# Second-layer attention of a hybrid decoder: which engine copies the turned tiles, how the projections are split, and a fourth output row begun early

## The chip, the cores and the metric

The kernel runs on one core of a Trainium2 chip. The metric is the device time of one execution in microseconds (us). The core's engines each have a queue of instructions that they take in order: PE (TensorE: matmuls, and transposes as matmuls), DVE (VectorE), ACT (ScalarE), POOL (GpSimd) and SP (SyncE, which here only issues transfers). An instruction that waits for a semaphore holds up all that stands behind it on its engine.

## The reference

The reference is a decoder of two layers on 512 tokens of width 1024: a gated delta-rule layer, then a layer with sliding-window attention. What matters here is the second layer's mixer and the output projection behind it:

```python
proj = h @ swa_w_q[bl]
q = apply_partial_rope(proj[..., :SWA_Q_W].reshape(b_sz, s_len, SWA_HEADS, SWA_DH), cos, sin)
mix_out = sliding_window_attention(q, shared_k, shared_v, swa_sinks[bl])
mem_q = proj[..., SWA_Q_W:]
...
mem_o = memory_attention(mem_q.reshape(b_sz, s_len, MEM_HEADS, MEM_DH), mem_k, mem_v)
x = x + jnp.concatenate([mix_out.astype(x.dtype), mem_o.astype(x.dtype)], axis=-1) @ w_out[layer]
x = x + swiglu(rms_norm(x, ln_ffn[layer]), w_gate_up[layer], w_down[layer])
```

and inside the attention, per block of 128 queries against the 256 keys of its own and the preceding block, twelve query heads on two key heads:

```python
m = jnp.maximum(jnp.max(s, axis=-1, keepdims=True), sink)
p = jnp.exp(s - m)
p = (p / (jnp.sum(p, axis=-1, keepdims=True) + jnp.exp(sink - m))).astype(v.dtype)
o = jnp.einsum("bnhgqk,bnkhd->bnqhgd", p, vw)
```

The memory attention has four heads and 256 fixed tokens, with no sinks.

## The kernel before

Activations lie with features on the 128 partitions and the 512 tokens along the free axis. A dense product is made exact to nearly float32 from rounded halves: `split` gives a high half (a copy on ACT, `whi`, `h`) and a low half (a subtraction on DVE, `wlo`, `l`), and `mm3` does three matmuls for each 128-row step k: high by high, high by low, low by high. So an output tile of 128x512 takes 8 steps or 24 matmuls, and every weight tile of 128x1024 is loaded to `wraw` by SP (two buffers), then split by ACT and DVE (three buffers `whi`/`wlo`) before PE can use it. A weight load waits until the tile that had its `wraw` buffer two loads earlier has been split.

The second layer's mixer is `swa`. Eight items t go through it: six head pairs (t = 0 to 5) and two pairs of memory heads (t = 6, 7). For each, `queries(t)` projects (24 matmuls into a `pj` bank of PSUM), `score(t)` makes the scores of four query blocks n = 0 to 3 into `qk` allocations of two banks each and DVE takes the maxima, `softmax(t)` makes the exponentials on ACT (for head pairs first the sinks' `es`, then eight of them into `sm`) and `weighed` scales and turns the probabilities and multiplies by the values. PSUM's eight banks are held as two `pj`, two `qk` allocations of two banks, and two `pt`.

`weighed` goes over the four blocks n. It scales the two halves b = 0, 1 of the block by the reciprocal of the sum (DVE for even n, ACT for odd n), turns the tile on PE into a `pt` bank (up to four 128x128 transposes), and copies the bank to SBUF as `pf`: on ACT, for n = 2 on DVE (L822). With all four turned, 28 matmuls (for memory items 4 wide ones) multiply by the values into another `pt` bank, and `split` of that bank gives the item's mix, `h` and `l`. It yields after n = 1 and n = 3, and ends with the product.

`beside(t, work)` drives `weighed` in three steps and puts dense work on PE in front of each: two k-steps of a projection (six matmuls), three times, so that PE has something to do while ACT and DVE scale and copy. The last two of the eight steps of the projection come after. In the loop's last two rounds and behind it, the dense work is that of the output projection: `row(1, m, ...)` is output tile m as a chain of eight steps in the order of items 6, 7, 0, 1, 2, 3, 4, 5, of which the last needs the mix of item 5. Rows 0, 1 (in `pj`) and 2 (in one half of a `qk` allocation) are begun in the attention. `output` then finishes these, makes the other rows (banks `pj`, `pj`, `pt` in turn, by m % 3), and behind each row adds it to the residual tile (`x`, on DVE), splits the result scaled by the gain as input of the feed-forward, and adds its square to the sum for the norm.

The feed-forward `ffn` starts with `gate(0)`: 24 matmuls into a `pj` bank. Its later tiles come in pairs by a scheme of seven products for eight, `quarters`, for which sums of weight tiles are needed: two `ws` loads of 256 KB on SP (L1020, L1021), onto which POOL adds two more of 256 KB by adding transfers (L1022, L1023), and a `wraw` load of 256 KB (L1025). `token_sums` makes sums of the inputs (`fc`, `raw`, `T`).

The order on each engine is not that of the Python code alone: the program's builder places instructions ahead where their inputs allow, loads and splits above all, keeping dependencies, buffers and the edges that `nosync` adds (an order on one engine without a semaphore). In the built program, loads and splits of rows 3 and 4 lie ahead of the end of the attention, and the `ws` loads of the feed-forward too.

Of the kernel before, what the change touches and what calls it, by code (L numbers as in the profile page):

```python
# [12 lines left out]
AF = mybir.ActivationFunctionType  # L13
ALU = mybir.AluOpType
# [4 lines left out]
P = 128  # L19
# [66 lines left out]
class Builder:  # L86
    def __init__(self, tc, a):
        self.tc, self.nc, self.a = tc, tc.nc, a
        self.n = 0
        self.valued = None  # L90
        self.table, self.table_ins, self.table_users = None, None, []


# [17 lines left out]
    def bank(self, tag, shape=(P, T)):  # L111
        return self.t(self.pp, list(shape), F32, tag, self.pbufs[tag])
# [278 lines left out]
    def gates(self, ep):  # L391
# [34 lines left out]
        self.mm(pg[:, NH:2 * NH], self.ones, g2)  # L426
        row = self.t(ep, [NH, P], F32, "row")
        self.copy(row, pg[:NH, 64:64 + P])
        dr = self.t(self.dpool, [1, NH * P], F32, "dr")
        nc.sync.dma_start(dr.rearrange("o (n i) -> (o n) i", i=P), row)  # L430
        self.dr = dr
        self.ngc = self.t(self.mpool, [P, NH], F32, "ngc")
# [356 lines left out]
    def weighed(self, pool, scores, vv, m, out, win):  # L789

        nc = self.nc
        own = "pt" in self.pbufs
        half = [slice(0, 64), slice(64, P)]
        sm, mx, den, nm = scores
        o = None if own else self.bank("sc")
        group = NC if own else 2
        for n in range(NC):
            if n % group == 0:
                pf = {} if win else self.t(pool, [P, 2, 2, group * P], F32, "pfm" if own else "pf", 1)
            k0 = 1 if win and n == 0 else 0  # L800
            p = sm[n][:, :, k0 * P:]
            dn = den.rearrange("p (b n) -> p n b", b=2)[:, n, :]
            for b in range(2):
                if n % 2:
                    self.copy(p[:, b], p[:, b], scale=dn[:, b:b + 1])
                else:
                    self.ts(p[:, b], p[:, b], dn[:, b:b + 1], ALU.mult)
            pt = self.bank("pt" if own else "g", [P, 2, 2, P])
            for j in range(k0, 2):
                for b in range(2):  # L810
                    turned = self.tr(pt[:, j, b, :], sm[n][:, b, j * P:(j + 1) * P])
                    if self.ahead is not None:

                        self.nosync(turned, self.ahead)
                        self.ahead = None
            if win:
                pf[n] = self.t(pool, [P, 2, 2, P], F32, "pf", group)
                to = pf[n][:, k0:]
            else:
                to = pf[:, :, :, n % group * P:(n % group + 1) * P]  # L820
            if own and n == 2:
                nc.vector.tensor_copy(to, pt[:, k0:])  # L822
            else:
                self.copy(to, pt[:, k0:])
            if own and n % 2:
                yield
            if (n + 1) % group:
                continue
            if own:
                o = self.bank("pt")  # L830
            if win:
                parts = [(t[:, j, b, :], vv[n - 1 + j][:, half[b]], slice(n * P, (n + 1) * P), j if n else 0, j, b)
                         for n, t in pf.items() for j in range(0 if n else 1, 2) for b in range(2)]
            else:
                parts = [(pf[:, j, b, :], vv[j][:, m * P + 64 * b:m * P + 64 * b + 64],
                          slice((n + 1 - group) * P, (n + 1) * P), j, j, b) for j in range(2) for b in range(2)]
            for t, v, s, first, end, b in parts:
                ins = self.mm(o[half[b], s], v, t, first == 0, end == 1)
                if turned is not None:
                    self.nosync(ins, turned)  # L840
                    turned = None
            self.valued = ins if own else None
        self.split(o, *out)


    def row(self, layer, m, mix, bank):

        w = self.weight(self.a["wout"][layer, m])
        for n, k in enumerate((6, 7, 0, 1, 2, 3, 4, 5)):
            if n:  # L850
                yield
            ps = bank() if n == 0 else ps
            self.mm3(ps, w, k, mix[k], n == 0, n == KD - 1)
        yield ps
# [259 lines left out]
    def swa(self, sp):  # L1114
        nc, a = self.nc, self.a
        memK, memV = self.fetch(sp, "mk"), self.fetch(sp, "mv")
        hk, h, qs, mix = [], [], {}, {}
        for t, base, pool in ((h, G_MIX[1], self.apool), (hk, G_KV, self.bpool)):
            for k in range(KD):
                t.append(self.pair(pool))  # L1120
                self.split_gain(self.x[k], self.gain(base, k), *t[k])
        sinks = self.small[:, 12:24].rearrange("p (b t) -> p t b", b=2)
        kk, vv = [], []

        def queries(t):
            w = self.weight(a["wq"][t])
            ps = self.bank("pj")
            for k in range(KD):
                self.mm3(ps, w, k, h[k], k == 0, k == KD - 1)
                yield  # L1130
            if len(qs) == 0:
                self.rstd_from(self.acc)
                for table in (self.cosT, self.sinT):
                    self.tt(nc.vector, table, table, self.rstd, ALU.mult)
            qs[t] = self.t(sp, [P, T], F32, "q", 3)
            if t < 6:
                self.rope(sp, ps, qs[t])
            else:
                self.tt(nc.vector, qs[t], ps, self.rstd, ALU.mult)

        def keys():
            kk.append(self.t(sp, [P, T], F32, "ks"))
            self.rope(sp, self.project(a["wkv"][0], hk), kk[0])

        def values():
            ps = self.project(a["wkv"][1], hk)
            v = self.t(sp, [P, T], F32, "rs", 2)
            self.tt(nc.vector, v, ps, self.rstd, ALU.mult)
            vv.append(v)

        def transpose_values():
            v = vv.pop()
            pt = self.bank("pt")
            for c in range(NC):
                self.tr(pt[:, c * P:(c + 1) * P], v[:, c * P:(c + 1) * P])
            vt = self.t(sp, [P, NC, P], F32, "vt")
            self.copy(vt.rearrange("p c i -> p (c i)"), pt)
            vv.extend(vt[:, c, :] for c in range(NC))

        def score(t):  # L1160
            got[t] = self.scores(sp, qs[t], kk[0] if t < 6 else memK[t - 6], t < 6)

        def softmax(t):
            self.softmax(sp, got[t], sinks[:, t, :] if t < 6 else None)

        def beside(t, work):

            out = self.pair(self.bpool)
            steps = self.weighed(sp, got[t], *((vv, t) if t < 6 else (memV, t - 6)), out, t < 6)
            for _ in range(3):  # L1170
                for _ in range(2):
                    next(work, None)
                next(steps, None)
            mix[t] = out

        def all_of(*works):
            for w in works:
                yield from w

        two = lambda: self.bank("qk", [P, 2, 2, 2 * P])[:, 0].rearrange("p a b -> p (a b)")  # L1180
        rows = [self.row(1, m, mix, (lambda: self.bank("pj")) if m < 2 else two) for m in range(3)]
        some = lambda m, n: (next(rows[m]) for _ in range(n))
        got = {}
        for t in (6, 7):
            list(queries(t))
        score(6)
        keys()
        values()
        score(7)
        transpose_values()  # L1190
        list(queries(0))
        softmax(6)
        list(queries(1))

        for t in range(6):
            score(t)
            work = queries(t + 2) if t < 4 else some(t - 4, 4)
            beside((6, 7, 0, 1, 2, 3)[t], work)
            list(work)
            softmax((7, 0, 1, 2, 3, 4)[t])  # L1200
        work = all_of(some(0, 2), some(1, 2), some(2, 6))
        beside(4, work)
        softmax(5)
        list(work)
        beside(5, all_of(some(0, 1), some(1, 1), some(2, 1)))
        return mix, rows

    def final(self, fp, squares, t):
# [85 lines left out]
```

## Time and profile before

| | us |
|---|---|
| median of three runs | 1168.45 (1167.78 to 1170.06) |
| the profiled execution | 1168.72 |
| its span, first to last instruction | 1166.9 |
| mean granted TensorE clock | 0.997 |
| attention passes with the tail of the last one | about 696 to 784 |
| output rows behind them | about 784 to 811 |
| last feed-forward and the final norm | about 811 to 1167 |

Times in the views are us from the start of the span. A row of a timeline has the start, the duration, the engine, the line of the kernel that recorded the instruction, its operation, output <- inputs by the program's names, shapes and count; in square brackets stands the idle time of the engine ahead of it and what ended that. Helper functions record most operations, so L144 is any matmul, L148 any transpose, L138 any copy on ACT, L132 any other activation, L151 any two-tensor operation, and the tile's name tells which it is. Matmuls are pipelined: the distance between starts is the pace, and the duration shown is longer. A row of the waits has the engine and tile that waited, whom it waited for, us in total, times, and the longest.

### The profile page before, as it was taken

The numbers are of one execution on the slowest core, as the hardware profiler recorded it, in microseconds if no ns is written. First come the engines' busy times: TensorE is split into PE (matmuls) and PEld (weight loads), VectorE is DVE, ScalarE is ACT, GpSimd is POOL, SyncE is SP. The second block draws the span as 40 slices with busy tenths as digits, with TensorE's granted clock in tenths as the row PEclk, the third lists the DMA queues.
The fourth block names the chain that finished last, engine by engine and source line by source line (L and its number), as shares of the span: only waits on it lengthen the run. The fifth ranks groups of instructions, "written<-read, shape, count | busy, mean of one in ns | idle before, by whom it ended". The sixth has DMA issues, their size and how long they took to land.

```text
span 1166.9 us, 19281 instructions
## 1 busy us (share of the span) xinstructions
PE 1140.4 (98%) x7330; PEld 994.3 (85%) x7330; DVE 833.5 (71%) x1558; ACT 630.5 (54%) x1250; POOL 83.1 (7%) x93
## 2 busy tenths in 40 slices
PE   7999999999999999999999999999999999999996
PEld 5878777877889998899998876778999988999986
DVE  5664886767788877488965777748788734889654
ACT  7569563366466642256643555864666422666433
POOL 0210000000011101011100000010011000111000
PEclk9999999999999999999999999999999999999998
DMA  8333341234557736367623421144477633676232
GB/s 306 117 107 116 123 135 64 89 93 163 171 128 181 181 103 163 116 165 182 163 77 99 132 77 38 55 101 129 107 189 183 154 99 106 168 177 166 76 99 84
DMA packets 72943, 151.20 MB, mean 130 GB/s; under 512 B 16732, under 2 KB 19444, under 8 KB 72852
## 3 DMA queue, kind: packets, MB, share of 16 engines
q1 hardware_dynamic: 61908, 130.06, 35.6%
q0 software_dynamic: 10944, 19.93, 10.8%
q8 instruction: 57, 0.93, 0.3%
q14 instruction: 34, 0.28, 0.1%
HBM read 143.00 MB, written 6.96 MB: 129 GB/s over the span
## 4 chain that ended last, share of the span: by engine, by line
PE 82%; DVE 10%; ACT 5%; DMA 1%; issue 1%; SPq 0%; DVEq 0%; ACTq 0%
PE pj L144 39%; PE g L144 38%; PE sc L144 4%; DVE wlo L151 2%; ACT sm L132 2%; DVE sm L750 1%; PE pt L144 1%; DVE big L151 1%; ACT whi L138 1%; DVE btmp L151 1%; PE g L148 1%; DMA wraw<-in_wmk 1%; ACT sm L138 1%; DVE q L151 1%; DVE qv L154 1%
## 5 line engine op out<-in xcount | busy, mean ns | idle before, releaser
L138 ACT ACTIVATE whi<-wraw 128x512 fp32r<-128x512 f32 (+3 forms) x325 | 243.3, 755 | 259.5 <-PE pj L144 154.5
L151 DVE TENSOR_TENSOR wlo<-wraw,whi 128x512 fp32r<-128x512 f32 (+3 forms) x325 | 272.7, 848 | 104.2 <-ACT whi L138 97.8
L144 PE MATMUL pj<-h,whi 128*128 128x512 f32 (+1 forms) x676 | 267.5, 397 | 1.1 <-ACT h L138 0.7
L144 PE MATMUL pj<-l,whi 128*128 128x512 f32 (+1 forms) x676 | 264.5, 391 | 0.0
L144 PE MATMUL pj<-h,wlo 128*128 128x512 f32 (+1 forms) x676 | 263.6, 391 | 0.5 <-DVE wlo L151 0.5
L144 PE MATMUL g<-T,whi 128*128 128x256 f32 x1216 | 220.5, 282 | 0.0
L144 PEld LDWEIGHTS g<-T,whi 128*128 128x128 f32 x1216 | 187.0, 189 | 1.1 <-DVE fu L154 1.1
L144 PE MATMUL g<-T,wlo 128*128 128x256 f32 x608 | 171.1, 281 | 0.0
L144 PEld LDWEIGHTS pj<-h,whi 128*128 128x128 f32 x676 | 126.9, 188 | 33.4 <-issue 6.2
L144 PEld LDWEIGHTS pj<-h,wlo 128*128 128x128 f32 x676 | 127.0, 188 | 27.1 <-DVE wlo L151 1.4
L144 PEld LDWEIGHTS pj<-l,whi 128*128 128x128 f32 x676 | 127.1, 188 | 25.6 <-issue 0.9
L144 PE MATMUL g<-h,whi 128*128 128x256 f32 (+1 forms) x500 | 146.6, 293 | 0.0
L144 PE MATMUL g<-h,wlo 128*128 128x256 f32 (+1 forms) x500 | 145.8, 292 | 0.0
L144 PE MATMUL g<-l,whi 128*128 128x256 f32 (+1 forms) x500 | 145.5, 291 | 0.0
L144 PEld LDWEIGHTS g<-T,wlo 128*128 128x128 f32 x608 | 114.4, 188 | 0.0
L144 PEld LDWEIGHTS g<-h,whi 128*128 128x128 f32 x500 | 94.9, 190 | 2.3 <-issue 0.5
L144 PEld LDWEIGHTS g<-l,whi 128*128 128x128 f32 x500 | 94.9, 190 | 2.3 <-issue 0.5
L144 PEld LDWEIGHTS g<-h,wlo 128*128 128x128 f32 x500 | 95.0, 190 | 1.8
L1022 POOL DMA_DIRECT2D ws<-in_wgu x38 | 33.3, 876 | 748.5 <-ACT h L138 246.8
L138 ACT ACTIVATE whi<-ws 128x512 fp32r<-128x512 f32 x76 | 48.1, 633 | 49.8 <-PE g L144 41.5
L151 DVE TENSOR_TENSOR fu<-pj,rstd 128x512 f32<-128x512 f32 (+1 forms) x34 | 22.4, 660 | 54.4 <-PE pj L144 54.4
L151 DVE TENSOR_TENSOR wlo<-ws,whi 128x512 fp32r<-128x512 f32 x76 | 52.2, 686 | 7.7 <-ACT whi L138 7.6
(367 smaller groups left out, 1647.5 us busy)
## 6 DMA issues: line engine op xcount, KB each, us to landing
wraw<-in_wgu SPq DMA_DIRECT2D x50, 512.0 KB, 4.0
ws<-in_wgu SPq DMA_DIRECT2D x76, 256.0 KB, 3.4
ws<-in_wgu POOLq DMA_DIRECT2D x76, 256.0 KB, 4.7
wraw<-in_win SPq DMA_DIRECT2D x26, 512.0 KB, 3.7
wraw<-in_wdn SPq DMA_DIRECT2D x32, 384.0 KB, 3.0
wraw<-in_wdn SPq DMA_DIRECT2D x32, 320.0 KB, 2.9
wraw<-in_wgu SPq DMA_DIRECT2D x38, 256.0 KB, 4.1
wraw<-in_wout SPq DMA_DIRECT2D x16, 512.0 KB, 3.7
```

The costliest lines, as they stand in the source:

```text
L132: ins = self.nc.scalar.activation(out, in_, func, **kw).ins
L138: self.copied = self.nc.scalar.activation(out, in_, AF.Copy, **kw).ins
L144: return self.nc.tensor.matmul(out, lhsT, rhs, start=start, stop=stop, skip_group_check=more).ins
L148: return self.nc.tensor.transpose(out, in_, self.ident[:k, :k]).ins
L151: return eng.tensor_tensor(out=out, in0=a, in1=b, op=op).ins
L154: self.nc.vector.scalar_tensor_tensor(out=out, in0=in0, scalar=scalar, in1=in1, op0=op0, op1=op1)
L750: nc.vector.tensor_tensor_reduce(out=sm[n][:, b, c0:], in0=ps[b][:, n - n0, c0:], in1=self.band[:, c0:], scale=1.0, scalar=NEG, op0=ALU.ad ...
L1022: nc.gpsimd.dma_start(s1, a22, accum_op=ALU.add)
```

## The change

There are three edits.

In `weighed`, the copy on DVE is that of n = 3 in place of n = 2; the copies of n = 0, 1, 2 are on ACT. Two order edges are added through `self.turned`, which holds an instruction for even and one for odd n: the first scaling on ACT of n = 3 stands behind ACT's copy of n = 2 of the same item, and the first scaling on DVE of the next item's n = 0 stands behind DVE's copy of n = 3. The scalings are recorded directly instead of by the helpers, so that their instruction can be named; they are the same operations.

`beside` takes three pieces of work with their own lengths. For projections these are 2, 3 and the remaining 3 steps (the last piece takes all that is left, with the projection's ending) in place of 2, 2, 2 and 2 behind. The order within `weighed`'s steps is unchanged: the first piece stands ahead of n = 0, 1, the second ahead of n = 2, 3, the third ahead of the product, as the Python code goes.

The fourth output row, m = 3, is begun in the attention too. It has weight tiles of its own, `oh` and `ol` (one buffer each in the attention's pool), and shares a two-bank `qk` allocation with row 2, which took one half of it before. Behind the last product 6 of its 24 matmuls are left. `output` makes only m = 4 to 7 anew, in `pj`, `pt`, `pj`, `pj` by the unchanged m % 3; before, m = 3 took a `pj` as well, so that the number of `pj` allocations in the stage falls by one and, with two banks taken in turn, every later `pj` allocation is the other bank.

The numbers of matmuls, vector and scalar operations and transfers are unchanged. In the built program, by its order alone: on PE an attention pass has 9 projection matmuls between the turns of n = 1 and n = 2 and 7 between those of n = 2 and n = 3 (before, 6 between n = 1 and n = 2, and n = 3 right behind n = 2), then 2 or 3 more ahead of the product, in the first two passes also 2 of the next projection. On ACT, ahead of the copy of n = 2, stand the next item's `es` and the first three of its exponentials. On SP, the load for row 6 stands ahead of the first `ws` load of the feed-forward, two `ws` loads, a `wraw` load of 256 KB and two more `ws` loads follow, and then the load for row 7; before, the `ws` loads stood ahead of the loads for rows 5, 6 and 7. On DVE, the split (`wlo`) of the feed-forward's second weight load stands ahead of the add into `x` of row 7, and `T`, `l`, `sqa`, three `raw` and one `fc` with it.

```diff
-                    self.copy(p[:, b], p[:, b], scale=dn[:, b:b + 1])
+                    ins = nc.scalar.activation(p[:, b], p[:, b], AF.Copy, scale=dn[:, b:b + 1]).ins
                 else:
-                    self.ts(p[:, b], p[:, b], dn[:, b:b + 1], ALU.mult)
+                    ins = nc.vector.tensor_scalar(out=p[:, b], in0=p[:, b], scalar1=dn[:, b:b + 1], scalar2=None, op0=ALU.mult).ins
+                if b == 0 and self.turned[n % 2] is not None:
+
+                    self.nosync(ins, self.turned[n % 2])
+                    self.turned[n % 2] = None
...
-            if own and n == 2:
-                nc.vector.tensor_copy(to, pt[:, k0:])
+            if own and n == 3:
+                self.turned[0] = nc.vector.tensor_copy(to, pt[:, k0:]).ins
             else:
                 self.copy(to, pt[:, k0:])
+                if own and n == 2:
+                    self.turned[1] = self.copied
...
-    def row(self, layer, m, mix, bank):
+    def row(self, layer, m, mix, bank, **kw):
 
-        w = self.weight(self.a["wout"][layer, m])
+        w = self.weight(self.a["wout"][layer, m], **kw)
...
-        def beside(t, work):
+        def beside(t, *works):
 
             out = self.pair(self.bpool)
             steps = self.weighed(sp, got[t], *((vv, t) if t < 6 else (memV, t - 6)), out, t < 6)
-            for _ in range(3):
-                for _ in range(2):
-                    next(work, None)
+            for work in works:
+                list(work)
                 next(steps, None)
             mix[t] = out
...
-        two = lambda: self.bank("qk", [P, 2, 2, 2 * P])[:, 0].rearrange("p a b -> p (a b)")
-        rows = [self.row(1, m, mix, (lambda: self.bank("pj")) if m < 2 else two) for m in range(3)]
-        some = lambda m, n: (next(rows[m]) for _ in range(n))
+        pair = []
+
+        def half(m):
+            if not pair:
+                pair.extend(x.rearrange("p a b -> p (a b)") for x in (lambda two: (two[:, 0], two[:, 1]))(
+                    self.bank("qk", [P, 2, 2, 2 * P])))
+            return pair[m]
+
+        own = dict(pool=sp, tags=("oh", "ol"), bufs=1)
+        rows = [self.row(1, m, mix, (lambda: self.bank("pj")) if m < 2 else (lambda m=m: half(m - 2)),
+                         **(own if m == 3 else {})) for m in range(4)]
+        some = lambda work, n: (next(work) for _ in range(n))
...
         for t in range(6):
             score(t)
-            work = queries(t + 2) if t < 4 else some(t - 4, 4)
-            beside((6, 7, 0, 1, 2, 3)[t], work)
-            list(work)
+            work, n = (queries(t + 2), (2, 3, 4)) if t < 4 else (rows[t - 4], (1, 1, 2))
+            beside((6, 7, 0, 1, 2, 3)[t], *(some(work, i) if i < 4 else work for i in n))
             softmax((7, 0, 1, 2, 3, 4)[t])
-        work = all_of(some(0, 2), some(1, 2), some(2, 6))
-        beside(4, work)
+        beside(4, some(rows[0], 2), some(rows[1], 2), some(rows[2], 3))
         softmax(5)
-        list(work)
-        beside(5, all_of(some(0, 1), some(1, 1), some(2, 1)))
+        for m, n in ((2, 3), (3, 3)):
+            list(some(rows[m], n))
+        beside(5, some(rows[3], 3), [list(some(rows[m], 1)) for m in range(2)], some(rows[2], 1))
         return mix, rows
```

More of the change, by code (lines that the diff above doesn't have):

```diff
@@ L89, in __init__ @@
         self.n = 0
-        self.valued = None
+        self.valued, self.turned = None, [None, None]
         self.table, self.table_ins, self.table_users = None, None, []
@@ L1164, in softmax @@
             self.softmax(sp, got[t], sinks[:, t, :] if t < 6 else None)
-        def beside(t, work):
+        def beside(t, *works):
             out = self.pair(self.bpool)
             steps = self.weighed(sp, got[t], *((vv, t) if t < 6 else (memV, t - 6)), out, t < 6)
-            for _ in range(3):
-                for _ in range(2):
-                    next(work, None)
+            for work in works:
+                list(work)
                 next(steps, None)
             mix[t] = out
-        def all_of(*works):
-            for w in works:
-                yield from w
-        two = lambda: self.bank("qk", [P, 2, 2, 2 * P])[:, 0].rearrange("p a b -> p (a b)")
-        rows = [self.row(1, m, mix, (lambda: self.bank("pj")) if m < 2 else two) for m in range(3)]
-        some = lambda m, n: (next(rows[m]) for _ in range(n))
+        pair = []
[8 more added lines that the diff above has]
+        some = lambda work, n: (next(work) for _ in range(n))
         got = {}
```

## The prediction, made blind

> **What bounds the kernel now.** I read the page first: busy shares and the chain of work that ended last.
>
> ```profile
> PE 1140.4 (98%) x7330; PEld 994.3 (85%) x7330; DVE 833.5 (71%) x1558; ACT 630.5 (54%) x1250; POOL 83.1 (7%) x93
> ...
> PE 82%; DVE 10%; ACT 5%; DMA 1%; issue 1%; SPq 0%; DVEq 0%; ACTq 0%
> ```
>
> PE (TensorE's matmuls) is never long idle and holds 82% of the chain. So the change is worth what it does to PE's gaps. Next I read the windows, cut at the places that the change touches: the attention passes (696 to 784 us), the output rows behind them (784 to 811), and the last feed-forward.
>
> ```profile
> 696.00:784.00 88.00, 82.55 (x578) 62.23 (x576) 58.09 (x207) 58.02 (x169) 2.62 (x3) 1.00 0.22 61
> 784.00:811.00 27.00, 27.00 (x119) 22.37 (x120) 23.06 (x35) 13.61 (x19) 0.86 (x1) 1.00 0.54 149
> 811.00:1167.00 356.00, 347.06 (x2342) 320.09 (x2341) 247.72 (x415) 172.02 (x307) 32.00 (x36) 0.99 0.51 133
> ```
>
> The columns are start and end, length, then busy us (and instructions) of PE, its weight loads, DVE, ACT and POOL, the clock, the DMA share and GB/s. The passes leave PE idle for 88.00 - 82.55 = 5.45 us; that is nearly all that this stage can give. In the rows behind them PE is full (27.00 of 27.00), while DVE is at 23.06 of 27 and the transfers have risen from 61 to 149 GB/s. What PE waits for is in the waits: in the passes, first by matmuls, then by weight loads; then from 784 us to the end.
>
> ```profile
> PE pt L144 <- DVE pf L822: 2.9, 4, 1.1
> ```
>
> ```profile
> PEld pt L144 <- DVE pf L822: 4.8, 5, 1.6
> ```
>
> ```profile
> PE g L144 <- ACT fg L141: 1.0, 1, 1.0
> PE pj L144 <- DVE wlo L151: 0.5, 1, 0.5
> ```
>
> The wait that stands out is that of the product with the values (28 matmuls into `pt`) for DVE's copy of the third turned tile (L822): 2.9 to 4.8 us. From 784 us on, in 383 us, PE waits 1.5 us in all, of which 1.0 lies far on. So nothing behind the attention absorbs a delay: what arrives late there lengthens the kernel by as much.
>
> **The change part by part.** *The copies and the split projections.* One pass, as PE, ACT and DVE have it now:
>
> ```profile
> 739.79 0.40 PE L144 MATMUL pj<-h,wlo 128*128 128x512 f32 x1
> 740.83 1.75 PE L144 MATMUL pt<-pf,vt 128*64 128x128 f32 x28 [0.64 <-DVE pf L822]
> ```
>
> ```profile
> 740.56 0.58 ACT L138 ACTIVATE pf<-pt 128x512 f32<-128x512 f32 x1
> 741.04 0.90 ACT L138 ACTIVATE sm<-sm,den 128x256 f32<-128x256 f32 x2
> 741.84 0.20 ACT L132 ACTIVATE es<-es 128x8 f32<-128x8 f32 x1
> ...
> 742.71 0.50 ACT L132 ACTIVATE sm<-sm,nm 128x256 f32<-128x256 f32 x1
> ```
>
> ```profile
> 740.09 0.68 DVE L822 COPY pf<-pt 128x512 f32<-128x512 f32 x1
> ```
>
> The last projection matmul starts at 739.79; at the pace of 0.23 (rows 810.13 and 810.36 below) the product could start at 740.02 and starts at 740.83, 0.8 us late. DVE's copy, late behind a 1.22 us weight split, held the bank. The change takes this wait away: up to 4.8 us over the passes, by the higher of the two rows. What is late next is the fourth tile's turn. Its scalings now stand on ACT behind the third tile's copy, and by the built program's order that copy stands behind the start of the next head pair's softmax: the exponential of the sinks, two 128x128 and one 128x256 exponential. These take from 741.84 to 742.71 + 0.50 = 743.21, 1.37 us. Then come copy 0.58 and two scalings 0.90, so 1.48 with ACT free and up to 2.85 behind the exponentials, against seven projection matmuls in front of the fourth turn, 7 x 0.23 = 1.6 us. A pass then waits 0 to 1.25 us. The exponentials start when the next scores' maxima are in, while PE still has nine matmuls (2.1 us) to do, so some of them will be done; I take 0.8, nearer the upper end, since ACT has all three copies now. Five passes: 4.0 (0 to 6.2). The product itself now waits for DVE's copy of the fourth tile, 0.68, behind two or three matmuls (0.5 to 0.7): 0 to 0.2 a pass, 0.8 in all at most; I take it. The sum is -4.8 + 4.0 + 0.8 = 0.0.
>
> *The fourth row.* Its first 18 matmuls move ahead of the last product. The tail today:
>
> ```profile
> 779.35 0.74 PE L144 MATMUL pj<-h,whi 128*128 128x512 f32 x2 [0.70 <-ACT h L138]
> ```
>
> ```profile
> 782.07 0.68 DVE L151 TENSOR_TENSOR x<-qk,x 128x512 f32<-128x512 f32 x1
> 782.66 1.22 DVE L151 TENSOR_TENSOR wlo<-wraw,whi 128x1024 fp32r<-128x1024 f32 x1
> ```
>
> The 0.70 for the last mix stays: nothing stands between product and rows there. The split at 782.66 for the old row 3 made PE wait 0.5 (the wait row above); its weights are now split in the attention, so -0.5 (0 if the next row's weights take its place). First term: **-0.5, between -5.3 and +1.7**.
>
> *What the fourth row moves.* One fewer allocation of the two `pj` banks flips their turns. The first gate matmul of the feed-forward had the bank that x6's add frees; now it has x7's.
>
> ```profile
> 810.13 0.39 PE L144 MATMUL pj<-h,wlo 128*128 128x512 f32 x1
> 810.36 0.39 PE L144 MATMUL pj<-h,whi 128*128 128x512 f32 x1
> ```
>
> ```profile
> 800.59 0.68 DVE L151 TENSOR_TENSOR x<-pt,x 128x512 f32<-128x512 f32 x1
> ...
> 807.55 1.22 DVE L151 TENSOR_TENSOR wlo<-wraw,whi 128x1024 fp32r<-128x1024 f32 x1
> 808.68 0.75 DVE L154 SCALAR_TENSOR_TENSOR l<-x,gains,h 128x512 fp32r<-128x512 f32 x1
> 809.35 0.69 DVE L151 TENSOR_TENSOR sqa<-sqa,sq 128x512 f32<-128x512 f32 x1
> 809.95 0.49 DVE L154 SCALAR_TENSOR_TENSOR raw<-x,minus,raw 128x256 f32<-128x256 f32 x1
> ...
> 812.71 0.69 DVE L151 TENSOR_TENSOR x<-pj,x 128x512 f32<-128x512 f32 x1
> ```
>
> The gate starts at 810.36 and x7's add ends at 812.71 + 0.69 = 813.40. With DVE as late as today the new wait is 813.4 - 810.36 = 3.0 us; with DVE free it is the add and a hop, 0.9 with the last matmul's drain (0.39 - 0.23). Behind the waiting matmul stands all of the feed-forward.
>
> DVE won't be as today, because the loads move too. Today:
>
> ```profile
> 767.03 0.33 SPq L1020 DMA_DIRECT2D ws<-in_wgu  x1
> ...
> 783.91 8.20 SPq L177 DMA_DIRECT2D wraw<-in_wout  x3
> ```
>
> ```profile
> q1 hardware_dynamic: 877, 2.15, 44.1%
> q0 software_dynamic: 288, 0.52, 21.2%
> ...
> wraw<-in_wout SPq DMA_DIRECT2D x3, 512.0 KB, 4.4
> ```
>
> ```profile
> L138 ACT ACTIVATE whi<-wraw 128x1024 fp32r<-128x1024 f32 x7 | 7.3, 1054 | 2.6 <-PE pj L144 2.6
> ```
>
> SP issued the feed-forward's `ws` loads from 767 us on, inside the attention, and then the rows' loads from 783.91. Now row 6's load stands ahead of the `ws` loads in SP's queue and waits for row 4's split, behind x2's add, which slides back by the 18 matmuls: 782.07 + 18 x 0.23 = 786.2, add 0.68, split 1.22: about 788.2. All four `ws` loads, one `wraw` load of 256 KB and POOL's four adding loads (issued as their halves land) fall in the same stretch, and row 7's load lies behind the five. The queue rows (packets, MB, share of 15 us, 778 to 793) give 2.15 / (0.441 x 15) = 0.325 MB per us for SP's loads and 0.52 / (0.212 x 15) = 0.164 for POOL's: 1.6 us for 512 KB, 0.8 for 256 KB, 1.6 for a 256 KB add. The 4.4 holds 2.8 beyond the 1.6 of its bytes; I count 1 of it ahead of the first byte. From 789.2: row 6 1.6, five small 4.0, row 7 1.6, two of the adds 3.2, so row 7 lands at about 799.6, before at 792 + 4.4 = 796. Row 7 doesn't make PE wait yet: halves 1.05 and 1.22 later, 801.9, and its matmuls begin 24 x 0.23 = 5.5 before 810.4. But the second gate load is released only by row 7's split. If every transfer runs without a gap, the work up to it is 10.4 + 0.8 (the last small load) + 1.6 + 1.6 + 3.2 (two more adds) = 17.6, to 806.8, and since the release comes at about 802 with the 4.4 of the row above, 806 to 807.7; with the first gate's load still running then (3.2 more) up to 811. On DVE x7's add now stands behind that load's split. So: landed 807.7 to 811, +1.05 +1.22, +2.73 for what stands between (l 0.67, sqa 0.60, three raw at 0.40, fc 0.26, each by start distances as from 808.68 on), +0.74 for the add: 813.4 to 816.7. The gate is late by **3.1 to 6.4; I take 5.6**, near the upper end, since a 512 KB load takes 4.4 here where its rate alone gives 1.6, so gaps are the rule. Below both ends lies 0.9, if the loads are in time.
>
> The Trainium skill ("DMA: Bandwidth & Descriptors", section "Anatomy of one DMA — SWDGE (gpsimd) path") has 2.0 us plus bytes over 436 GB/s, an estimate of 3.2 us for 512 KB, where the row has 4.4 in this crowd; by it the loads would be in time sooner and the sum would be nearer +2.5.
>
> **Sum.** -0.5 + 5.6 = +5.1. The profiled execution took 1168.72 us (span 1166.9 and 1.8 around it), 0.27 over the median; against the median 1168.45 + 5.1 = **1173.5**.
>
> **The rivals.** *Bank alone:* the loads land early enough and DVE is as late as today: -0.5 + 3.0 = +2.5, 1171.0. For it: row 7 itself isn't late. Against it: the five loads have nowhere else to go. *In time:* DVE too catches up, since row 3's split left this stretch, and only 0.9 is left: +0.4, 1168.9. Against it: DVE's 23.06 of 27. *Faster:* as that, and the exponentials are done before the third copy on ACT, so all of the waits go: -5.3 + 0.9 + 0.8 = -3.6, 1164.9. It decides if ACT's backlog at the third turn stays under 0.1 us (1.6 - 1.48). For it: ACT is 54% busy; against it: the 1.37 us that the order puts in front. *Adds in the way:* POOL's four adds share evenly with SP's queue, so that all of them end ahead of row 7's load, 3.2 later; row 7 lands at 802.8, and the second gate load with it: +5.1 + 3.2 = +8.3, 1176.8. For it: POOL's adds move at half of SP's rate already.
>
> The Trainium skill speaks for this one: the same page, section "SWDGE vs HWDGE vs iDMA", says that POOL's and SP's transfers feed different queues within each engine, which it serves in turn; that queue 0's share is 21.2% beside 44.1% agrees with both being served together.
>
> **How the numbers follow.** A measurement of this kernel tells 0.2% (2.3 us) from no change. Forecast 0.50 (own range 1171.5 to 1176), adds in the way 0.15, bank alone 0.15, in time 0.14, faster 0.06. The range 1168.0 to 1179.0 leaves out the faster case, a quarter of "in time" and the dear end of the adds. Faster: 0.06 and 0.01 of "in time". No change (1166.1 to 1170.8): 0.13 and 0.06 of "bank alone". Slower: the rest, 0.74.
>
> **What would show it.** In the waits of the passes L822's row shrinks and scaled tiles on ACT (`pt` of L148 for `sm`) come in, about 4 us together. The stretch from the first scores to the last product is as long as now within a few us. PE waits for the add into x7, 3 to 6 us, at the first gate. Row 6's load is issued near 788 with the `ws` loads right behind it, and row 7's near 793. I am wrong if no wait of over 1 us stands at the first gate, or if the fourth turns wait for nothing.

## The result, and the profile after

The changed kernel takes 1173.78 us (median of five runs, 1172.70 to 1174.14) against 1168.45 (five runs, 1167.66 to 1170.06): the ratio is 1.0042 with a 95% interval of 1.0027 to 1.0057. That is 5.3 us more, where 5.1 was forecast (1173.5, range 1168.0 to 1179.0). The profiled execution took 1174.01 us, its span 1171.8, 4.9 more than before. The other 0.4 lies outside the span: 2.2 us around it, before 1.8. All the kernels below with four rows have 2.2 there and those with three 1.8 to 1.9; no run shows why.

The busy shares of the page hardly tell the two kernels apart, and the chain gives PE 86% in place of 82%:

```profile
PE 86%; DVE 8%; ACT 4%; DMA 1%; issue 1%; SPq 0%; DVEq 0%; ACTq 0%
```

The windows do, with the same cuts and columns as before:

```profile
696.00:784.00 88.00, 83.56 (x582) 62.89 (x581) 54.66 (x201) 55.98 (x167) 0.00 (x0) 1.00 0.14 43
784.00:811.00 27.00, 24.52 (x106) 19.31 (x104) 22.24 (x33) 15.85 (x22) 3.49 (x4) 0.99 0.71 195
```

The passes are as full as they were. The rows behind them have lost the 27.00 of 27.00 on PE, POOL has moved four adding loads into this stretch, and the transfers have risen from 149 to 195 GB/s. The waits of PE in the passes, by matmuls and by weight loads, and then from 788 us to the end:

```profile
PE pt L148 <- ACT sm L805: 2.5, 5, 0.6
PE pt L148 <- ACT pf L138: 0.9, 1, 0.9
```

```profile
PEld pt L148 <- ACT sm L805: 6.0, 8, 1.1
```

```profile
PE pj L144 <- DVE x L151: 5.2, 1, 5.2
PE g L144 <- ACT fg L141: 1.0, 1, 1.0
```

The wait for DVE's copy (2.9 by matmuls) is gone, with two smaller ones (0.5 for `nm`, 0.4 for `pfm`), and the turns (L148) wait for ACT instead, 2.5 + 0.9 = 3.4. And one wait of 5.2 us is new, for the add into x7. Here it is in PE's timeline:

```profile
813.96 0.77 PE L144 MATMUL pj<-h,whi 128*128 128x512 f32 x1 [5.23 <-DVE x L151]
814.53 0.63 PE L144 MATMUL pj<-l,whi 128*128 128x512 f32 x1
...
817.09 0.61 PE L144 MATMUL pj<-l,whi 128*128 128x512 f32 x1
...
821.19 1.02 PE L144 MATMUL g<-sqa,consts 128*128 128x512 f32 x2
```

Behind it the matmuls start 0.43 us apart ((817.09 - 814.53) / 6), where the pace before and after this stretch is 0.23. The windows over the wait, the stretch behind it and the next one give the granted clock in the column behind POOL: 0.51 in the second. It fell during the wait already: 0.68 on average over the first.

```profile
808.90:813.90 5.00, 0.00 (x0) 0.00 (x0) 5.00 (x10) 2.28 (x5) 0.00 (x0) 0.68 0.34 105
813.90:817.60 3.70, 3.64 (x9) 2.89 (x10) 3.70 (x5) 2.14 (x3) 0.00 (x0) 0.51 0.29 75
817.60:822.00 4.40, 4.40 (x20) 3.32 (x18) 2.08 (x6) 0.84 (x1) 0.00 (x0) 1.00 0.14 58
```

To compare executions, the first scores of the attention are a better origin than the start of the span. The code ahead of them is the same, and yet they stand at 698.06 in the one trace and at 696.50 in the other (695.8 to 697.8 in the ten kernels below). Before, then after, the first scores, the first matmul behind the last mix (after; the prediction shows it for before at 779.35) and the sum of squares that follows the first gate:

```profile
698.06 1.79 PE L144 MATMUL qk<-ks,q 64*128 64x128 f32 x16 [0.24 <-DVE q L151]
...
815.84 1.13 PE L144 MATMUL g<-sqa,consts 128*128 128x512 f32 x2
```

```profile
696.50 1.79 PE L144 MATMUL qk<-ks,q 64*128 64x128 f32 x16 [0.22 <-DVE q L151]
...
782.40 0.73 PE L144 MATMUL pj<-h,whi 128*128 128x512 f32 x2 [0.70 <-ACT h L138]
```

From these, and with 18 matmuls at 0.228 = 4.10 us moved ahead of the mark at the tail:

| stretch | before | after | difference |
|---|---|---|---|
| start of the span to the first scores | 698.06 | 696.50 | -1.56 |
| first scores to the matmul behind the last mix, without the 18 | 81.29 | 85.90 - 4.10 = 81.80 | +0.51 |
| from there to the end of row 7 (with the 18) | 810.36 - 779.35 = 31.01 | 813.96 - 5.23 - 782.40 + 4.10 = 30.43 | -0.58 |
| wait at the first gate | 0 | 5.23 | +5.23 |
| first gate's 24 matmuls | 815.84 - 810.36 = 5.48 | 821.19 - 813.96 = 7.23 | +1.75 |
| from there to the end | 351.06 | 350.61 | -0.45 |

The sum is +4.90, the difference of the spans; from the first scores on it is +6.46. The loss stands at one place: 5.23 of waiting and 1.75 of slow matmuls behind it.

### The profile page after: what moved, and what is told of

It reads as the page before. It is cut to its first block, busy times and chain, and to the rows that moved or that the text cites. A ratio compares the mean times of both kernels' runs of the same rounds, so it can differ in the third digit from the quotient of the medians.

```text
span 1171.8 us, 19281 instructions
## 1 busy us (share of the span) xinstructions
PE 1143.1 (98%) x7330; PEld 995.9 (85%) x7330; DVE 832.6 (71%) x1558; ACT 628.9 (54%) x1250; POOL 83.0 (7%) x93
## 3 DMA queue, kind: packets, MB, share of 16 engines
q0 software_dynamic: 10944, 19.93, 10.9%
## 4 chain that ended last, share of the span: by engine, by line
PE 86%; DVE 8%; ACT 4%; DMA 1%; issue 1%; SPq 0%; DVEq 0%; ACTq 0%
PE pj L144 40%; PE g L144 38%; PE sc L144 5%; DVE wlo L151 2%; ACT sm L132 1%; DVE sm L750 1%; PE qk L144 1%; PE g L148 1%; DMA wraw<-in_wgu 1%; PE pt L144 1%; DMA wraw<-in_wmk 1%; PE pt L148 1%; ACT sm L805 1%; DVE qv L154 1%; DVE q L151 0%
## 5 line engine op out<-in xcount | busy, mean ns | idle before, releaser
L138 ACT ACTIVATE whi<-wraw 128x512 fp32r<-128x512 f32 (+2 forms) x324 | 241.9, 753 | 270.9 <-PE pj L144 162.6
L151 DVE TENSOR_TENSOR wlo<-wraw,whi 128x512 fp32r<-128x512 f32 (+2 forms) x324 | 270.5, 843 | 109.3 <-ACT whi L138 103.9
L144 PE MATMUL pj<-h,whi 128*128 128x512 f32 (+1 forms) x668 | 264.6, 397 | 6.1 <-DVE x L151 5.2
```

Source lines behind the costliest of these rows:

```text
L138: self.copied = self.nc.scalar.activation(out, in_, AF.Copy, **kw).ins
L144: return self.nc.tensor.matmul(out, lhsT, rhs, start=start, stop=stop, skip_group_check=more).ins
L151: return eng.tensor_tensor(out=out, in0=a, in1=b, op=op).ins
```

## Experiments

Each kernel was timed in five rounds beside the kernel before on the same chip, and its ratio is that of its runs to those of before, with a 95% interval. The table has, for every trace, the distance from the first scores to the first matmul behind the last mix and to the sum of squares behind the first gate. In kernels with four rows, the first distance holds the 4.10 us of the 18 matmuls. Each kernel has one trace. The five kernels with the same passes (the change, other bank, other load order, bank and loads, add ahead of the split) give 85.85 to 85.90 to the last mix, so this distance repeats to about 0.1 us.

| kernel | median us (before beside it) | ratio | to the last mix | to the sum of squares |
|---|---|---|---|---|
| before | | | 81.29 | 117.78 |
| the change | 1173.78 (1168.45) | 1.0042 (1.0027 to 1.0057) | 85.90 | 124.69 |
| three rows | 1167.94 (1167.75) | 0.9996 (0.9987 to 1.0005) | 81.26 | 119.39 |
| fourth row alone | 1173.60 (1167.75) | 1.0045 (1.0032 to 1.0058) | 84.97 | 124.51 |
| other bank | 1169.33 (1167.75) | 1.0009 (1.0001 to 1.0018) | 85.89 | 119.47 |
| other load order | 1170.16 (1167.75) | 1.0015 (1.0007 to 1.0024) | 85.86 | 121.94 |
| bank and loads | 1167.47 (1168.20) | 0.9991 (0.9983 to 1.0000) | 85.85 | 117.46 |
| split projections alone | 1168.60 (1168.20) | 0.9997 (0.9987 to 1.0008) | 80.90 | 119.46 |
| copies alone | 1169.43 (1168.20) | 1.0010 (1.0001 to 1.0019) | 82.66 | 120.10 |
| bank and loads, old copies | 1166.17 (1168.20) | 0.9988 (0.9979 to 0.9996) | 85.76 | 117.39 |
| add ahead of the split | 1174.47 (1169.10) | 1.0036 (1.0022 to 1.0050) | 85.88 | 124.71 |
| bank and loads, mixed copies | 1166.86 (1169.10) | 0.9980 (0.9971 to 0.9990) | 85.33 | 116.94 |

### Which edit it is: three rows, and the fourth row alone

The first kernel keeps the copies and the split projections, and begins three rows:

```diff
-        rows = [self.row(1, m, mix, (lambda: self.bank("pj")) if m < 2 else (lambda m=m: half(m - 2)),
-                         **(own if m == 3 else {})) for m in range(4)]
+        rows = [self.row(1, m, mix, (lambda: self.bank("pj")) if m < 2 else (lambda m=m: half(m - 2)))
+                for m in range(3)]
...
-        for m, n in ((2, 3), (3, 3)):
-            list(some(rows[m], n))
-        beside(5, some(rows[3], 3), [list(some(rows[m], 1)) for m in range(2)], some(rows[2], 1))
+        list(some(rows[2], 3))
+        beside(5, [], [list(some(rows[m], 1)) for m in range(2)], some(rows[2], 1))
```

> The changed kernel with three rows begun in the attention, as before; copies, order edges and the split projections stay changed. My theory (all of the loss stands at the first gate, the passes give nothing and take nothing): 1167.0 to 1170.0 us, no wait of PE for the add into x7, the first scores to the tail as long as in the kernel before within 1 us. Rival, the passes lose (new waits for scaled tiles on ACT, 2.5 us by matmuls and 6.0 by weight loads, come on top): 1171 us or more. Rival, the passes gain and the fourth row hides it: under 1166.

The second is the kernel before with the fourth row, its `half`, `own` and `rows` as in the change, and its first six steps ahead of the last item:

```diff
         list(work)
+        list(some(3, 6))
         beside(5, all_of(some(0, 1), some(1, 1), some(2, 1)))
```

> The kernel before with the fourth row alone: begun in the attention with six steps and weight tiles of its own; copies and projections as before. My theory: 1172.0 to 1175.0 us, PE waits 4 to 6 us for the add into x7 at the first gate, slow matmuls behind it. Rival, the copies and split projections make the loss: 1167.5 to 1169.5 us and no such wait.

The waits from 790 us on, of three rows and then of the fourth row alone, without the 1.0 for `fg` that every kernel has:

```profile
PE pj L144 <- DVE l L154: 0.5, 1, 0.5
PE pj L144 <- ACT h L138: 0.5, 1, 0.5
```

```profile
PE pj L144 <- DVE x L151: 5.5, 1, 5.5
```

With three rows the kernel is as fast as before, and PE waits for no add. The two waits of 0.5 are of the gate's last step, for the halves of x7: DVE is late there too, but another bank is free. This trace is of the slowest of its executions (1170.07) and is 1.6 us behind the kernel before at the sum of squares, which the median doesn't show. The fourth row alone gives the whole loss, by the same wait. The rivals that the passes lose, or gain what the row then hides, fall.

### What makes the wait: the bank, the loads, the order on DVE

Row 7 in a `pt` bank. Nothing else moves on any engine:

```diff
-        bank = lambda m: self.bank(("pj", "pj", "pt" if begun else "g")[m % 3])
+        bank = lambda m: self.bank("pt" if begun and m == 7 else ("pj", "pj", "pt" if begun else "g")[m % 3])
```

> The changed kernel with row 7 in a pt bank in place of a pj bank, so that the first gate matmul takes the bank that the add into x4 frees; all else, the loads and the orders of ACT, DVE, POOL and SP among it, is unchanged. My theory in its strict form (the bank turns lateness on DVE into a wait): the wait of 5.2 us goes, the gate starts some 5 us earlier against the first scores, and only its last step waits for the halves of x7, about 1 us (x7's add 813.8, halves 1.4 later, step due 4.8 after 808.7): 1168 to 1170.5 us. Rival, the late loads alone decide whatever the bank: the wait moves to that last step nearly whole, 3 us or more, 1171.5 to 1173.5 us.

Order edges that put the feed-forward's `ws` and small `wraw` loads behind row 7's load on SP (`rowed` is the load of the last row; the `wraw` load has the same edge):

```diff
-        nc.sync.dma_start(s1, a21)
-        nc.sync.dma_start(s3, a11)
+        for s, part in ((s1, a21), (s3, a11)):
+            ins = nc.sync.dma_start(s, part).ins
+            if self.rowed is not None:
+                self.nosync(ins, self.rowed)
```

> The changed kernel with one order edge more: the ws and small wraw loads of the last feed-forward stand behind row 7's load in SP's queue; the bank stays flipped, and on DVE the second weight split still stands ahead of the add into x7. If the loads make most of the wait: row 7's load lands near 795 to 796 in place of 798.5, PE waits 1 to 3 us for the add into x7, 1169 to 1171.5 us. If the bank and DVE's order alone make it: the wait stays at 4 us or more, 1172.5 to 1174 us.

The waits from 790 us on, again without `fg`, with the other bank and then with the other load order:

```profile
PE pj L144 <- DVE l L154: 0.9, 1, 0.9
PE pj L144 <- ACT h L138: 0.5, 1, 0.5
```

```profile
PE pj L144 <- DVE x L151: 2.6, 1, 2.6
```

With the other bank the gate starts on time though x7's add is still late: it ends 116.6 us behind the first scores, in the change 117.3, before 115.3. What is left is 0.9 + 0.5 at its last step, and no slow matmul: 5.2 us less to the sum of squares (124.69 to 119.47), 1.7 more than before. With the loads in the other order the wait is halved, and slow matmuls stand behind it still (the gate's 24 take 7.16 us, before 5.48). Here x7's add ends 114.6 us behind the first scores, a little earlier than before, and the 2.6 left is near the 3.0 that the prediction gave to the bank with DVE as late as before. So each remedy takes part away. Both together:

> The changed kernel with both remedies: row 7 in a pt bank, and the feed-forward's ws loads behind row 7's load in SP's queue. My theory (bank and loads together are the whole loss): no wait of PE for x7's add, and the last step of the first gate hardly waits for x7's halves (add done about 2.6 us behind the row, halves 1.4 later, step due 4.8 behind it): 1166.5 to 1168.8 us, 1 us or more under the kernel with the bank alone. Rival, something else of the changed order costs too: 1169.5 us or more.

The wait and the last step's waits are gone, and the distance to the sum of squares is 117.46, 0.3 under the kernel before. The time, 1167.47, is 0.9991 of before with an interval that ends at 1.0000. Bank and loads are the whole loss.

What the late loads do to DVE can be read in the trace of the change. ACT's and then DVE's timeline:

```profile
798.59 1.06 ACT L138 ACTIVATE whi<-wraw 128x1024 fp32r<-128x1024 f32 x1 [3.60 <-DMA wraw<-in_wout]
803.03 1.06 ACT L138 ACTIVATE whi<-wraw 128x1024 fp32r<-128x1024 f32 x1 [3.38 <-DMA wraw<-in_wgu]
...
808.01 1.04 ACT L138 ACTIVATE whi<-wraw 128x1024 fp32r<-128x1024 f32 x1
```

```profile
799.69 1.23 DVE L151 TENSOR_TENSOR wlo<-wraw,whi 128x1024 fp32r<-128x1024 f32 x1 [2.65 <-ACT whi L138]
...
804.12 1.23 DVE L151 TENSOR_TENSOR wlo<-wraw,whi 128x1024 fp32r<-128x1024 f32 x1 [1.82 <-ACT whi L138]
...
809.28 1.22 DVE L151 TENSOR_TENSOR wlo<-wraw,whi 128x1024 fp32r<-128x1024 f32 x1
...
813.13 0.69 DVE L151 TENSOR_TENSOR x<-pj,x 128x512 f32<-128x512 f32 x1
```

ACT waits 3.60 us for row 7's load and 3.38 for the first gate's, and DVE waits 2.65 and 1.82 behind it. The second wait is the one that counts: what row 7's load had cost DVE ended in it. The first gate's load was issued at 794.87, when row 6's weights had been split, and ACT took it up at 803.03, 8.2 us later; with the other load order it landed 5.2 us after its issue. The split of the second gate load at 809.28, which the prediction held to be the late one, follows without idle time: that load was issued at 800.94 and landed 5.1 us later, at 806.0. From 804.12 to the add DVE has one gap of 0.26 us and is simply behind. One more kernel tells the two readings apart; it puts that split behind the add:

```diff
+            self.hold = self.added if layer and f0 == 0 else None
+            w = self.weight(col(f0, 1))
+            self.hold = None
...
+        if self.hold is not None:
+            self.nosync(ins, self.hold)
```

> The changed kernel with one order edge on DVE: the split of the feed-forward's second weight load stands behind the add into x7 and no longer ahead of it; the loads and the bank stay as changed. Theory of the prediction (that load's landing sets the add's time): the add no longer waits for it and comes soon after row 7's last matmul: the wait falls from 5.2 us to 1 to 3 us, 1169.5 to 1171.5 us. Theory from the trace (the load has landed in time, and DVE is behind because it waited 2.65 and 1.82 us earlier for the halves of row 7 and of the first gate): the add comes sooner only by the split's own 1.1 us, the wait is 4.0 to 4.4 us, 1172 to 1173.5 us.

Its waits, and DVE's timeline:

```profile
PE pj L144 <- DVE x L151: 4.4, 1, 4.4
```

```profile
808.39 1.23 DVE L151 TENSOR_TENSOR T<-raw,T 128x1024 fp32r<-128x1024 f32 x1 [0.27 <-ACT T L138]
...
812.77 0.68 DVE L151 TENSOR_TENSOR x<-pj,x 128x512 f32<-128x512 f32 x1
813.37 1.21 DVE L151 TENSOR_TENSOR wlo<-wraw,whi 128x1024 fp32r<-128x1024 f32 x1
```

The wait falls by 0.8 us, not to 1 to 3: the second load doesn't set it, DVE's lag does. It is less than the split's 1.1 because the built order now has one `raw` (0.4) more ahead of the add. The time expected for that case was missed upwards, 1174.47 for 1172 to 1173.5: the slow matmuls last longer here, and to the sum of squares nothing is won (124.71 for 124.69).

### What the passes do: copies and split, each alone

The split projections with the third tile's copy on DVE as before and no edges, and the copies with edges but with the projections as before; three rows in both.

> The projections in three parts alone: three rows, the third tile's copy on DVE, no order edges. By the built program's order n = 2 and n = 3 are turned together again and nine projection matmuls (2.05 us) stand ahead of the product in place of six. If the wait for DVE's copy (0.8 us in the pass shown, 4.8 in all by weight loads) is only a matter of cover: three matmuls more, 0.7 us a pass, take most of it, the first scores to the tail shrink by 2.5 to 4.5 us and the time is 1164 to 1166.5 us. Rival, what was waited for comes back ahead of the turns (scaled tiles): 1167 to 1169 us.

> The copies and the order edges alone: three rows, projections 2, 2, 2 and 2 behind. If three copies on ACT with the fourth scalings behind them make the new wait (ACT needs 1.5 us and more between the third copy and the fourth turn): the passes are 1 to 4 us longer than before and PE waits for scaled tiles of ACT: 1168.5 to 1172 us. Rival, they are what gains, and the split loses it: under 1166.5 us.

The waits of PE in the passes, the split alone and then the copies alone:

```profile
PE pt L148 <- ACT pf L138: 2.7, 3, 1.5
```

```profile
PE pt L148 <- ACT sm L805: 3.9, 6, 1.1
```

The split alone does take the wait for DVE's copy away, and in the first four rounds 1.5 us are won (the fifth scores stand 44.5 us behind the first, before 46.0). But the two `pt` banks then wait for ACT's copies in the later rounds (2.7 us), and to the tail only 0.4 is left of the 2.5 to 4.5 expected; its rival, that the wait comes back ahead of the turns, is what happened, though by ACT's copies and not by scaled tiles. At the gate's last step it then waits for x7's halves (to the sum of squares 1.7 more than before), and the time is unchanged. The clock falls there too, to 0.50 from 816 to 819 us, and this trace is of the slowest of its executions (1169.80). The copies alone cost 1.4 us in the passes and 0.1% in time: ACT is asked for the fourth scalings with only the pair of turns in between. Together, in the kernel with three rows, the two come to -0.03 to the tail, where -0.4 and +1.4 would add to +1.0; why they don't add is not shown.

### Versions under both kernels

With both remedies, four rows and split projections, first with DVE's copies, then with DVE's copies for the memory items and head pairs 0 and 1 and ACT's for head pairs 2 to 5 (the edit is the second's):

```diff
-            if own and n == 3:
-                self.turned[0] = nc.vector.tensor_copy(to, pt[:, k0:]).ins
+            late = own and win and m > 1
+            if own and n == (3 if late else 2):
+                ins = nc.vector.tensor_copy(to, pt[:, k0:]).ins
+                if late:
+                    self.turned[0] = ins
```

> Both remedies at the first gate, four rows and the projections in three parts, but the third tile's copy on DVE and no order edges. If the copies on ACT cost the passes what the split gains: 1163.5 to 1166.5 us, under both kernels. Rival, the split gains nothing: 1166.5 to 1169 us, as with both remedies alone.

> Both remedies at the first gate, four rows, the projections in three parts, and the third tile's copy on DVE for the memory items and head pairs 0 and 1, on ACT with the order edges for head pairs 2 to 5. From the distances of the first scores: with DVE's copies the first four rounds take 44.5 us against 46.4, with ACT's copies the rest to the tail takes 39.5 us against 41.3 (four rows in both). If the two parts add: the first scores to the tail 84.0 us, 1.8 less than in either, and 1164 to 1166 us, under the best so far (1166.2). Rival, what one part gains the next one loses: 85.5 us and 1166 to 1167.5 us.

Both come out a little under the kernel before, at 0.9988 and 0.9980 of it. The old copies' 1166.17 lies in the range expected if the split gains, but the trace doesn't bear that out: to the tail they win 0.09 us over ACT's copies (85.76 for 85.85), and the interval overlaps that of both remedies alone. The mixed copies, at 1166.86, missed 1164 to 1166 and win 0.4 us to the tail over the old ones, not 1.8, as their rival had it. Their first four rounds take 44.1 us against 46.4 with ACT's copies; the fifth then takes 10.9 against 8.3, with waits of 0.86 (for the mix's `l` on DVE) and 1.53 (for ACT's copy). That is the round in which the copies change over, but the old copies, which don't change, have waits of 0.46 and 1.53 there too, so the change-over is not shown to be the cause. With the old copies the clock also fell in that round:

```profile
747.05:750.20 3.15, 3.14 (x12) 2.86 (x13) 2.74 (x13) 1.43 (x3) 0.00 (x0) 0.50 0.54 166
```

The two medians were not taken beside the same runs of before, so they are compared by their ratios, whose intervals overlap.

## Why the prediction was right

**The place and the sign.** The forecast put the loss at the first gate: a bank that x7's add frees in place of x6's, loads that slide behind the tail, and nothing behind that could absorb it. All three are shown: the bank alone removes the wait, the load order alone halves it, and from 788 us on PE's only other wait is the 1.0 that was there before.

**Passes.** Forecast 0.0 from -4.8 + 4.0 + 0.8, measured +0.51. That it came near is in part luck. The 4.0 for scaled tiles came to 2.5 by matmuls (0.5 a pass for 0.8), the 0.8 for the product's own wait came to nothing, and 0.9 for a bank that ACT's copy held was in no term. Nor do the waits make up the +0.51: PE's idle time from the first scores to the tail fell from 4.48 to 4.22 us, and its busy time without the 18 matmuls grew from 76.81 to 77.58; why is not shown. A pass of the change, ACT and then PE:

```profile
738.65 0.49 ACT L132 ACTIVATE sm<-sm,nm 128x256 f32<-128x256 f32 x1
...
739.14 0.58 ACT L138 ACTIVATE pf<-pt 128x512 f32<-128x512 f32 x1
739.62 0.50 ACT L805 ACTIVATE sm<-sm,den 128x256 f32<-128x256 f32 x1
```

```profile
740.17 0.66 PE L148 MATMUL pt<-consts,sm 128*128 128x128 f32 x4 [0.62 <-ACT sm L805]
```

The copy did stand behind nearly all of the exponentials (I had held that some would be done), but only one scaling lies between copy and turn, not two: only the half b = 0 has the edge, and the other is done earlier.

**Row 3's split.** Forecast -0.5, measured -0.58 between the tail and the end of row 7, and the 0.5 wait for `wlo` there is gone.

**The loads.** Moved to the origin of before (+1.56), row 7's load was issued at 793.5, forecast 793, and taken up by ACT at 800.2, forecast to land at 799.6. The rows, SP's queue and then the load's time to landing:

```profile
787.37 0.38 SPq L1026 DMA_DIRECT2D ws<-in_wgu  x1
...
791.91 0.33 SPq L177 DMA_DIRECT2D wraw<-in_wout  x1
```

```profile
wraw<-in_wout SPq DMA_DIRECT2D x1, 512.0 KB, 6.6
```

It took 6.6 us, and 3.6 in the kernel with the other load order. The 3.2 us given by the estimate from the Trainium skill ("DMA: Bandwidth & Descriptors", section "Anatomy of one DMA — SWDGE (gpsimd) path") is close to the second and far from the first; the page fits it to transfers that GpSimd issues, and these are SP's. So the crowd nearly doubled it, but row 7's own matmuls still did not wait.

**The gate.** Forecast 5.6, measured 5.23; the size was right, partly by luck, for a step behind it was not. I had taken the second gate load to land at 807.7 to 811 and to hold up DVE by its split. It landed at 806.0, on the origin of before 807.6, and DVE was not yet free for its split. With that landing the forecast's own chain (+1.05 +1.22 +2.73 +0.74) gives 813.3 and a wait of 3.0. (The range of 3.1 to 6.4 began at 807.7, the upper end of the case without gaps; its lower end, 806, would have given 1.4.) The other 2.2 is DVE's backlog from the late load of the first gate, which the sum did not hold; it took the place of a late landing. The kernel with the add ahead of the split shows that the second load does not set the wait. With the other load order it does hold DVE up, by 1.46 us.

**What was not in the sum.** The slow matmuls behind the wait, +1.75, were in no term. The start of that execution, -1.56, happened to hide them in the spans; it is in code that the change doesn't touch. From the first scores on, the change is 6.46 us longer in these two traces, against 5.3 by the medians and 5.1 forecast. So that the total came this near is luck in part; the place and the sign are not.

**The rivals.** The bank alone (with DVE as late as before, 1171.0), in time, and faster fall by the wait of 5.2 and by ACT's waits in the passes. Adds in the way: POOL's four adds were issued from 792.19 on, behind row 7's load, and the last at 796.50, 2 us before that load had landed. They landed 7.3 to 8.2 us after their issue, from 799.5 on, so none of them ended ahead of it, where that rival had all four. They moved beside the first gate's load instead.

## What to carry to other kernels

Work that is begun early for one stage moves everything that was tied to its old place: count the buffer and bank turns behind it, and follow each queue past which its loads slide, before looking at the matmuls. When a full engine loses time at one point, look for the pair of causes: here a bank made a lag into a wait, and late loads made the lag; either remedy alone gave part of the time back, both gave all of it. A mean share of 22 of 27 us busy can hide a stretch without room: from its last wait to the add, DVE had 0.26 us free in 9.7 and could not catch up.

## What the runs showed of the hardware that was not expected

After some waits of PE, the matmuls behind them run at about half pace. The granted clock was 0.51 for 3.7 us after the wait of 5.2 in the change. With the other load order a wait of 2.6 us was enough; the two windows are the wait and the stretch behind it:

```profile
808.20:810.80 2.60, 0.02 (x1) 0.01 (x1) 2.60 (x7) 1.15 (x2) 0.00 (x0) 1.00 1.00 234
810.80:814.40 3.60, 3.58 (x9) 2.86 (x10) 3.60 (x5) 2.10 (x3) 0.00 (x0) 0.56 0.42 105
```

With the old copies, waits of 0.46 and 1.53 within 3.4 us were enough (0.50 from 747.05 to 750.2), and with the split projections alone waits of 0.93 and 0.54 at the gate (0.50 from 816 to 819). Yet with the mixed copies, after waits of 0.86 and 1.53 in the same round, the clock stayed at 1.00, and so it did with the other bank, after 0.46 and 0.93 at the gate. So the length of the waits alone doesn't decide, and no run here shows what does. The Trainium skill ("TensorE: Matmul & The Clock Gate", section "Part 1: The HAM clock gate (the "warmup" mystery)") has half rate after an idle window of about 3.4 us, and full rate again after about as long a busy one. The halving agrees, and so does the slow stretch of 3.7 us (in the kernel with the add ahead of the split it was 5.2); the idle time needed was shorter here. So a wait of PE can cost more than itself, here 1.75 us on top of 5.23.
